# One derived weight of a transformed causal convolution, moved from VectorE to a ScalarE copy and an accumulating DMA

## The chip, the core and the metric

The kernel runs on one core of a Trainium2 chip. The metric is device time in microseconds (us), the median of several executions. TensorE (PE in the profile, with its weight loads listed apart as PEld) multiplies matrices into PSUM; VectorE (DVE) and ScalarE (ACT) do elementwise work; GpSimd (POOL) issues most loads, and SyncE (SP) issues stores and transposing transfers. The engines run their own instruction lists in order and wait for one another through semaphores.

## The reference

```python
def setup_inputs():
    B, S, D, K = 8, 4096, 512, 8
    ...x: (B, S, D) float32, kernel: (K, D, D) float32...

def reference(x, kernel):
    out = np.zeros_like(x)
    for k in range(K):
        if k == 0:
            shifted = x
        else:
            shifted = np.concatenate([np.zeros((B, k, D), dtype=np.float32), x[:, :-k, :]], axis=1)
        out += np.matmul(shifted, kernel[k])
    return out.astype(np.float32)
```

It is a causal convolution over the sequence with eight taps, where each tap is a 512x512 matrix: eight shifted copies of x, each multiplied by its own matrix, are added up.

## The kernel before

The sequences are cut into 128 runs, one to a partition, of 256 positions each. A run is worked off in 32 steps of K = 8 positions. In each step an 8x8 Toeplitz product of 512x512 blocks is to be formed, and the kernel saves multiplications in the manner of Karatsuba, three levels deep: a step has three nodes, `LO`, `HI` and `MID`, instead of four quarter products, and within a node the same is done twice more. For this it needs weights that are differences of taps. There are 27 weight tiles `W[a, b, c]`, each index one of `LO`, `HI`, `MID`, and each tile 128 partitions by 4x512 values in bf16 (512 KB). Eight of them are the taps themselves, loaded by `load_w`, with the cast from float32 in the transfer. A tile with a `MID` in it is the difference of two others, formed on VectorE by `mid_dve(level, u, v)`; the function `mid` gives the result and the two operands. `mid_dve(0, HI, LO)` forms `W[MID,HI,LO] = W[HI,HI,LO] - W[LO,HI,LO]`. Three readers come after it: `mid_dve(1, MID, LO)` at L469 (which gives `W[MID,MID,LO]`), `mid_dve(2, MID, HI)` (which gives `W[MID,HI,MID]`), and the product `node_l(nodes[4], 1, LO)` on TensorE.

x is loaded in halves of four positions by `load_x(i, h)` into a pool of two buffers named `xin`, issued by GpSimd with a cast to bf16. It is transposed into `XT`, in the first steps by TensorE (`transpose_pe`), later by a transposing DMA (`transpose_x`, issued by SP). A load into a buffer waits until the transposes that read the buffer's former content are done: `load_x(2, 1)` at L421 waits for `transpose_x(1, 1)`. VectorE forms the sums of positions in `D4`, `D42`, `D421` and so on, which TensorE takes as its stationary operand.

A node is a series of products of four matmuls each (`product`, L191): `node_a1` and `node_a0` (weights `W[a, MID, ...]`), `node_u`, `node_v` (weights `W[a, b, MID]`) and `node_l`. In between, ScalarE copies PSUM halves (`node_seed`, `node_dts`, the copy in `node_a1`), and VectorE subtracts in PSUM (`node_d`, L76 or L266). `node_l(n, b, HI)` adds to the half that `node_d(n, b)` has read, so it waits for that `node_d`.

The order of all instructions is written by hand (`tc.manual_schedule()`): each engine works off its part of the program text in the order written. The text of the first two steps (six nodes, L330 to L560 or so) mixes products, weight differences, sums and loads one by one, because in this stretch the weights are still arriving or being formed. From the third step on a regular loop follows. The names of all elementwise lines in the profile are those of helpers: L76 is `tt`, every tensor-tensor operation on VectorE, whatever it computes. The profile's `w` is any weight tile.

The first two steps also use some weight tiles that are still free as scratch (`E4`, `T4`, `T42`, `C0`, `C1`). `W[MID,HI,LO]` and its two operands are not among these.

Of the kernel before, what the change touches and what calls it, by code (L numbers as in the profile page):

```python
# [18 lines left out]
LO, HI, MID = 0, 1, 2  # L19
# [3 lines left out]
def kernel(  # L23
# [6 lines left out]
    nc = tc.nc  # L30
# [10 lines left out]
    ADD = mybir.AluOpType.add  # L41
# [14 lines left out]
    W = {}  # L56
# [18 lines left out]
    def tt(o, a, b, op):  # L75
        nc.vector.tensor_tensor(out=o, in0=a, in1=b, op=op)  # L76


    def load(out, src):
        nc.gpsimd.dma_start(out=out, in_=src)  # L80
# [3 lines left out]
    def load_x(i, h):  # L84
        xin[i, h] = xpool.tile([P, 4, D], bf, name="xin")
        load(xin[i, h], xr[:, K * i + 4 * h:K * i + 4 * h + 4, :])
# [31 lines left out]
    def prep_d42(h):  # L118
        if h == LO:
            tt(pairs(D42)[:, 0:2], pairs(D4)[:, 3::-3], pairs(D4)[:, 0:2], ADD)  # L120
        else:
            tt(D42[:, 4:8], D4[:, 2:6], D4[:, 4:8], ADD)
# [11 lines left out]
    def pair(k):  # L134
        return ppool.tile([P, 2, D], f32, name=f"pp{k}")
# [13 lines left out]
    def load_w(tap):  # L149
        n = K - 1 - tap  # L150
        load(W[n >> 2, n >> 1 & 1, n & 1], kr[:, :, tap, :])

    def mid(level, u, v):

        if level == 0:
            return W[MID, u, v], W[HI, u, v], W[LO, u, v]
        if level == 1:
            return W[u, MID, v], W[u, HI, v], W[u, LO, v]
        return W[u, v, MID], W[u, v, LO], W[u, v, HI]

    def mid_dve(*which):
        o, u, v = mid(*which)
        tt(o, u, v, SUB)

    load_w(4)
    load_h(-7, -4)
# [9 lines left out]
    def transpose_pe(name, k, src, t0, t1):  # L176
        o = pair(k).bitcast(bf).rearrange("p a (b d) -> p (a b) d", b=2)
        for t in range(t0, t1):
            for c in range(DC):
                nc.tensor.transpose(o[:, t - t0, c * P:(c + 1) * P], src[:, t, c * P:(c + 1) * P],  # L180
                                    ident)
        bank[name] = o[:, 0:t1 - t0]
# [75 lines left out]
    def node_v(n, b_):  # L258
        product(n.p[b_][:, 1], n.s[2][b_], W[n.a, b_, MID], False)

    def node_d(n, b_):
        p = n.p[b_]
        if b_ == LO:
            tt(p[:, 0], n.dts, p[:, 1], SUB)
        else:
            nc.vector.scalar_tensor_tensor(out=p[:, 0], in0=p[:, 1], scalar=-1.0,  # L266
                                           in1=n.dts, op0=MUL, op1=SUB)
# [48 lines left out]
    def direct(m, t):  # L316
        n = K // 2 - 1 - m
        product(n0.p[t // 2][:, t % 2], D4[:, t - m] if t >= m else E4[:, 4 + t - m],
                W[LO, n >> 1, n & 1], m == 0)
# [42 lines left out]
    tt(D1, XF[:, 3:5], XF[:, 4:6], ADD)  # L362
    direct(1, 2)
    mid_dve(1, LO, HI)
    load_x(1, 0)
    direct(1, 1)
    mid_dve(2, LO, HI)
    tt(F21, D2[:, 0:4], D2[:, 1:5], ADD)
    load_w(0)
    mid_dve(1, LO, LO)  # L370
    mid_dve(2, LO, LO)
    direct(2, 3)
    mid_dve(2, LO, MID)
    transpose_pe("x1", 2, xin[0, 1], 0, 4)
    nc.vector.tensor_copy(out=XT[:, 4:8], in_=bank["x1"])  # L375
    tt(D4[:, 4:8], XF[:, 4:8], XT[:, 4:8], ADD)
# [42 lines left out]
    node_l(nodes[1], 0, HI)  # L419
    node_v(nodes[1], 1)  # L420
    load_x(2, 1)  # L421
    node_d(nodes[1], 1)
    mid_dve(2, HI, MID)
    prep_d421(HI)
# [19 lines left out]
    node_a1(3)  # L444
    node_l(nodes[2], 0, LO)
    mid_dve(0, LO, LO)
    mid_dve(0, HI, LO)
    prep_d42(HI)
    node_l(nodes[2], 0, HI)
    node_a0(nodes[3])  # L450
# [182 lines left out]
```

## Time and profile before

| what | value |
|---|---|
| time, median of 4 runs | 782.47 us (781.68 to 782.84) |
| the profiled execution | 782.99 us, span of its instructions 781.1 us |
| busy, PE | 765.1 us (98% of the span), 3505 matmuls recorded |
| busy, DVE | 660.6 us (85%) |
| busy, ACT | 280.7 us (36%) |
| busy, POOL | 41.8 us (5%) |
| DMA | 138.37 MB, mean 177 GB/s |
| mean granted TensorE clock | 0.993 |

The span is what lies between the first and the last instruction; the profiled execution's own time is 1.9 us more. Busy time of PE is the sum of modelled instruction spans, and following matmuls overlap in it, so a busy share of 98% doesn't mean that PE has only 2% to win or lose. The stretches of interest are the first 65 us; after it the loop repeats with each step of three nodes.

### The profile page before, as it was taken

How to read it: one execution, taken by the hardware profiler on the slowest of the kernel's cores; microseconds unless marked ns; L12 is line 12 of the kernel's file. 1: busy time of each engine (PE TensorE's matmuls, PEld its weight loads, DVE VectorE, ACT ScalarE, POOL GpSimd, SP SyncE). 2: the span in 40 equal slices, each digit the busy share in tenths (PEclk: the TensorE clock that was granted, in tenths of full speed). 3: DMA queues.
4: the chain of work that ended last, by engine and by line, in shares of the span. 5: the costliest groups of instructions: out<-in, count | busy, mean ns of one | idle time of the engine just before them, and what ended most of it. 6: DMA issues, size and time to landing. Idle time of an engine off the chain costs nothing.

```text
span 781.1 us, 9348 instructions
## 1 busy us (share of the span) xinstructions
PE 765.1 (98%) x3505; PEld 348.7 (45%) x3576; DVE 660.6 (85%) x768; ACT 280.7 (36%) x459; POOL 41.8 (5%) x80
## 2 busy tenths in 40 slices
PE   7999999999999999999999999999999999999997
PEld 3444444444444444444444444444444444444443
DVE  3999988888888898888898888888888898888895
ACT  1453433333343324343333333333343333343332
POOL 4000000000000000000000000000000000000000
PEclk7999999999999999999999999999999999999999
DMA  9946978777787787787687787878697867788843
GB/s 163 210 79 154 246 169 212 172 179 173 178 177 196 174 185 176 172 190 187 163 196 178 165 202 176 198 159 187 168 189 178 206 163 186 164 181 179 205 130 124
DMA packets 159229, 138.37 MB, mean 177 GB/s; under 512 B 130130, under 2 KB 134226, under 8 KB 159184
## 3 DMA queue, kind: packets, MB, share of 16 engines
q1 hardware_dynamic: 145312, 98.84, 45.7%
q0 software_dynamic: 13728, 38.66, 30.7%
q8 instruction: 28, 0.46, 0.2%
q10 hardware_dynamic: 144, 0.26, 0.1%
q14 instruction: 17, 0.14, 0.1%
HBM read 77.32 MB, written 67.11 MB: 185 GB/s over the span
## 4 chain that ended last, share of the span: by engine, by line
PE 91%; DVE 5%; DMA 2%; issue 1%; ACT 0%; DVEq 0%; POOL 0%; SPq 0%; ACTq 0%; POOLq 0%
PE pp L191 91%; DVE D L76 2%; DVE w L76 2%; DMA XT<-xin 1%; DMA xin<-in_x_dram 1%; DVE y L76 1%; PE pp L180 1%; DVE pp L76 0%; DVE pp L266 0%; DVE XT L375 0%; ACT D L341 0%; ACT D L342 0%; DVE D L334 0%; POOL D L80 0%; DVEq L628 0%
## 5 line engine op out<-in xcount | busy, mean ns | idle before, releaser
L191 PE MATMUL pp<-w,D 128*128 128x512 bf16 x3213 | 714.4, 380 | 5.8 <-ACT D L342 1.2
L191 PEld LDWEIGHTS <-D 128*128 128x128 bf16 x3280 | 320.7, 98 | 392.4 <-issue 5.6
L76 DVE TENSOR_TENSOR D<-D 128x1024 bf16<-128x1024 bf16 x252 | 228.4, 946 | 0.4 <-issue 0.2
L76 DVE TENSOR_TENSOR y<-pp,ms 128x1024 f32<-128x1024 f32 (+1 forms) x121 | 146.4, 1211 | 45.7 <-PE pp L191 44.1
L76 DVE TENSOR_TENSOR D<-XT 128x2048 bf16<-128x2048 bf16 (+2 forms) x153 | 142.3, 946 | 12.3 <-DMA XT<-xin 10.7
L238 ACT COPY pp<-pp 128x512 f32<-128x512 f32 x95 | 54.1, 570 | 254.9 <-PE pp L191 252.1
L250 ACT COPY pp<-pp 128x512 f32<-128x512 f32 x95 | 54.2, 571 | 163.7 <-PE pp L191 151.7
L76 DVE TENSOR_TENSOR pp<-dts,pp 128x512 f32<-128x512 f32 x95 | 65.5, 690 | 43.1 <-ACT dts L256 41.8
L293 ACT COPY ms<-pp 128x1024 f32<-128x1024 f32 x60 | 61.0, 1016 | 34.9 <-PE pp L191 30.6
L80 POOL DMA_DIRECT2D xin<-in_x_dram x64 | 33.9, 530 | 690.7 <-DMA XT<-xin 673.4
L266 DVE SCALAR_TENSOR_TENSOR pp<-pp,dts 128x512 f32<-128x512 f32 x95 | 65.9, 693 | 3.3
L256 ACT COPY dts<-pp 128x512 f32<-128x512 f32 x95 | 57.5, 606 | 4.2 <-PE pp L191 4.2
L252 ACT ACTIVATE pp<-pp 128x512 f32<-128x512 f32 x95 | 56.0, 589 | 2.1 <-DVE D L76 2.1
L191 PE MATMUL pp<-w,XT 128*128 128x512 bf16 x118 | 30.5, 379 | 0.1
L76 DVE TENSOR_TENSOR w<-w,w 128x2048 bf16<-128x2048 bf16 x19 | 22.6, 1218 | 0.0
L191 PEld LDWEIGHTS <-XT 128*128 128x128 bf16 x120 | 11.7, 98 | 14.2
L191 PE MATMUL pp<-w,w 128*128 128x512 bf16 x34 | 8.8, 379 | 0.8 <-ACT pp L250 0.7
L191 PE MATMUL pp<-w,F 128*128 128x512 bf16 x36 | 8.6, 379 | 0.0
L174 PE MATMUL pp<-zero 128*128 128x512 bf16 x16 | 6.3, 554 | 1.2 <-DVE zero L145 1.2
L180 PE MATMUL pp<-ident,xin 128*128 128x128 bf16 x48 | 4.2, 249 | 3.1 <-DMA xin<-in_x_dram 1.9
L334 DVE COPY D<-pp 128x1024 bf16<-128x1024 bf16 x1 | 0.7, 691 | 7.1 <-PE pp L180 7.1
L378 ACT COPY w<-XT 128x1024 bf16<-128x1024 bf16 x1 | 1.0, 1045 | 14.3 <-DVE XT L375 14.3
(52 smaller groups left out, 74.9 us busy)
## 6 DMA issues: line engine op xcount, KB each, us to landing
out_dram<-y SPq DMA_DIRECT2D x123, 512.0 KB, 3.3
xin<-in_x_dram POOLq DMA_DIRECT2D x64, 512.0 KB, 5.5
w<-in_kernel_dram POOLq DMA_DIRECT2D x8, 512.0 KB, 16.6
out_dram<-ms SPq DMA_DIRECT2D x2, 512.0 KB, 6.6
out_dram<-f SPq DMA_DIRECT2D x2, 512.0 KB, 9.0
XT<-xin SPq DMA_TRANSPOSE x61, 6.2
D<-in_x_dram POOLq DMA_DIRECT2D x1, 508.0 KB, 5.5
D<-in_x_dram POOLq DMA_DIRECT2D x1, 381.0 KB, 11.1
```

The lines of the kernel that those rows point to most:

```text
L76: nc.vector.tensor_tensor(out=o, in0=a, in1=b, op=op)
L80: nc.gpsimd.dma_start(out=out, in_=src)
L174: nc.tensor.matmul(pw[:, h], lhsT=zero[:, 0:P], rhs=zero, start=True, stop=True)
L180: nc.tensor.transpose(o[:, t - t0, c * P:(c + 1) * P], src[:, t, c * P:(c + 1) * P], ident)
L191: nc.tensor.matmul(bank, lhsT=comp[:, c * P:(c + 1) * P], rhs=w[:, c, :], start=start and c == 0, stop=c == DC - 1, skip_group_check=True)
L238: nc.scalar.copy(out=n.q[:, 0], in_=n.q[:, 1])
L250: nc.scalar.copy(out=n.p[b_][:, 1], in_=n.q[:, 1])
L252: nc.scalar.mul(out=n.p[b_][:, 1], in_=n.q[:, 1], mul=-1.0)
L256: nc.scalar.copy(out=n.dts, in_=n.q[:, 0])
L266: nc.vector.scalar_tensor_tensor(out=p[:, 0], in0=p[:, 1], scalar=-1.0, in1=n.dts, op0=MUL, op1=SUB)
L293: nc.scalar.copy(out=ms[b_], in_=p)
L378: nc.scalar.copy(out=C0[:, 0:2], in_=XT[:, 6:8])
```

## The change

`mid_dve(0, HI, LO)` is taken out of VectorE's list. In its place there are two instructions. ScalarE writes the negated `W[LO,HI,LO]` into `W[MID,HI,LO]`, at a place in the text just before the first transposes of `xin[0, 1]`. Later GpSimd issues one DMA, from SBUF to SBUF, that adds `W[HI,HI,LO]` to what stands in `W[MID,HI,LO]`; it stands in the text right behind `load_x(2, 1)`, so GpSimd gets to it once that load has been issued, which is once the transposes of the second step's upper half (`transpose_x(1, 1)`) are done. The weight comes out the same: `W[HI,HI,LO] - W[LO,HI,LO]` in bf16.

```diff
     def mid_dve(*which):
         o, u, v = mid(*which)
         tt(o, u, v, SUB)
+
+
+    def mid_neg(u, v):
+        nc.scalar.mul(out=W[MID, u, v], in_=W[LO, u, v], mul=-1.0)
+
+    def mid_acc(u, v):
+        nc.gpsimd.dma_start(out=W[MID, u, v], in_=W[HI, u, v], accum_op=ADD)
 ...
     mid_dve(2, LO, LO)
     direct(2, 3)
     mid_dve(2, LO, MID)
+    mid_neg(HI, LO)
     transpose_pe("x1", 2, xin[0, 1], 0, 4)
 ...
     node_v(nodes[1], 1)
     load_x(2, 1)
+    mid_acc(HI, LO)
     node_d(nodes[1], 1)
 ...
     mid_dve(0, LO, LO)
-    mid_dve(0, HI, LO)
     prep_d42(HI)
```

## The prediction

> **What bounds the kernel now.** I read the page first, its busy shares and its chain of work by engine.
>
> ```profile
> PE 765.1 (98%) x3505; PEld 348.7 (45%) x3576; DVE 660.6 (85%) x768; ACT 280.7 (36%) x459; POOL 41.8 (5%) x80
> PE 91%; DVE 5%; DMA 2%; issue 1%; ACT 0%; DVEq 0%; POOL 0%; SPq 0%; ACTq 0%; POOLq 0%
> ```
>
> TensorE carries nine tenths of the chain, so a removed VectorE instruction is worth only what TensorE stops waiting for. VectorE's 5% lies in one stretch, which the chain in order of time shows (start, length, what), here cut to 45 to 66 us:
>
> ```profile
> 48.73 2.26 DVE w L76 x2
> 50.99 1.14 DVE D L76
> 52.12 0.06 DVE pp L266
> 52.18 0.46 issue
> 52.64 1.21 DVE D L76
> 53.85 1.14 DVE w L76
> 54.99 0.33 DVE A L76
> 55.32 1.15 DVE w L76
> 56.47 0.05 issue
> 56.52 3.63 PE pp L191 x16
> ```
>
> Up to 56.5 VectorE leads and TensorE follows; from there TensorE leads, with 0.05 us pieces that recur every 10.8 us to the end and so hang on no dependency. The instruction to be removed is the second of the pair at 48.73. How long TensorE really waits is in the stage table by single microseconds (PE, PEld, DVE, ACT, POOL busy, clock, DMA share, GB/s):
>
> ```profile
> 48.00:49.00 1.00, 0.83 (x4) 0.41 (x5) 1.00 (x3) 0.00 (x0) 0.00 (x0) 1.00 1.13 229
> 52.00:53.00 1.00, 0.88 (x5) 0.29 (x3) 1.00 (x3) 0.97 (x2) 0.00 (x0) 1.00 0.00 0
> 56.00:57.00 1.00, 0.88 (x5) 0.25 (x4) 1.00 (x3) 0.56 (x1) 0.00 (x0) 1.00 0.03 8
> 62.00:63.00 1.00, 0.95 (x5) 0.23 (x4) 1.00 (x2) 1.00 (x3) 0.00 (x0) 1.00 0.50 92
> ```
>
> A visible gap is smaller than the delay, because listed matmuls overlap. TensorE's timeline gives the rate: 16 in a row last 3.62 us, so with 0.379 us for the last one, 15 steps take 3.24 us, 0.216 us each; 0.379 - 0.216 = 0.163 us of each step is overlap.
>
> ```profile
> 23.07 3.62 PE L191 MATMUL pp<-w,D 128*128 128x512 bf16 x16
> ```
>
> So the gaps of 0.12, 0.12 and 0.05 us at 52.8, 56.5 and 62.8 delay TensorE by about 0.28, 0.28 and 0.21 us. The gap at 48 lies ahead of the removed instruction and stays.
>
> **What is removed.** VectorE's timeline:
>
> ```profile
> 48.63 2.35 DVE L76 TENSOR_TENSOR w<-w,w 128x2048 bf16<-128x2048 bf16 x2
> 57.58 1.22 DVE L76 TENSOR_TENSOR w<-w,w 128x2048 bf16<-128x2048 bf16 x1
> 61.50 2.36 DVE L76 TENSOR_TENSOR w<-w,w 128x2048 bf16<-128x2048 bf16 x2
> ```
>
> Two take 2.35 us, one 1.22, so the second is worth 1.13 us of VectorE's time. VectorE has no idle time from there to 65 us, so everything behind moves up by 1.13 us while its inputs allow.
>
> Follow the waits. At 52.79 `node_l(nodes[2], 1, HI)` waits for `node_d(nodes[2], 1)`, which ended at 52.04 + 0.69 = 52.73 and now ends near 51.6; TensorE gets there at 52.79 - 0.28 = 52.51. Gone: 0.28. At 56.52 `node_a1(4)` waits for `W[MID,MID,HI]` (55.24 + 1.22 = 56.46), now ready at 55.33; TensorE arrives at 56.52 - 0.56 = 55.96. Gone: another 0.28. At 62.78 `node_v(nodes[4], 0)` waits for `W[MID,LO,MID]`, first of the pair at 61.50, now done near 61.6, while TensorE arrives at 62.78 - 0.21 - 0.56 = 62.0. But this product also needs the seed copy, which ends on ScalarE at 61.96 + 0.58 = 62.54 and moves up only with TensorE, by 0.56, to about 61.98. So little is kept there: I count 0.15 of 0.21. What is late next is TensorE itself; two small waits behind (its weight loader's waits for `F` near 73.3 and 75.9, some 0.1 us each) may lose 0.04. Sum: 0.28 + 0.28 + 0.15 + 0.04 = 0.75 us.
>
> **The negated copy.** ScalarE's timeline:
>
> ```profile
> 28.88 1.04 ACT L378 COPY w<-XT 128x1024 bf16<-128x1024 bf16 x1 [14.25 <-DVE XT L375]
> 31.95 1.90 ACT L391 COPY w<-XT 128x2048 bf16<-128x2048 bf16 x1
> ```
>
> A copy of this shape takes 1.90 us. It stands in ScalarE's list just ahead of the copy at 28.88, before which ScalarE idles 14.25 us. It waits for tap 5, which VectorE already reads in the pair of differences that starts at 20.66, so it runs at about 22 to 24 us at the latest, 5 us before anything queued behind it. Counted at nothing. Without that cover it would hold up the copies of `XT` behind it by up to 1.9 us, and with them VectorE's `T4` sum.
>
> **The accumulating DMA.** GpSimd's timeline:
>
> ```profile
> 45.29 0.53 POOL L80 DMA_DIRECT2D xin<-in_x_dram  x1 [14.50 <-DMA XT<-xin]
> 63.62 0.53 POOL L80 DMA_DIRECT2D xin<-in_x_dram  x1 [17.80 <-DMA XT<-xin]
> ```
>
> It is issued at 45.82 and takes 0.5 to 0.8 us of GpSimd (`load_x` and `load_w` rows). It waits for the copy (done by 24) and for tap 1, whose load left at 17.06 and lands in at most 20.6 us, 37.7. Only `load_x(3, 0)` is queued behind it, at 63.62 after 17.80 us of idling: nothing. The transfer follows `load_x(2, 1)` on the same queue:
>
> ```profile
> DMA  0000000099992547499891989939699190000000
> xin<-in_x_dram POOLq DMA_DIRECT2D x1, 512.0 KB, 4.9
> ```
>
> This is the DMA view of 45.5 to 50.5 us in slices of 0.125: the load moves from 46.5 to 49.6 (3.1 us) and lands at 45.29 + 4.9 = 50.2. Then the DMA engines are idle until the transposes issued at 58.77 (the 52 to 53 row above has 0 GB/s). No row shows an accumulate. Lower bound: it runs beside the load as quickly as a 512 KB store, 3.3 us, landing at 49.1. Upper bound: it starts when the load has landed and takes twice its 4.9, because the destination is read too: 50.2 + 9.8 = 60.0. The load row is nearest, since it also reads 1 MB (float32) and writes 512 KB: 49.6 + 3.1 + 0.6 for landing = 53.3.
>
> The first reader is `mid_dve(1, MID, LO)`, at 57.58 before, now due at 56.45. A landing by 56.85 costs nothing (the 0.4 us that `W[MID,LO,MID]` has over TensorE); at 57.58 VectorE is where it was before and the gain is lost at 62.78; from there each microsecond late costs one, since VectorE's whole list queues behind that wait. At 53.3 there are 3.5 us to spare: nothing.
>
> The Trainium skill has a price for the add: Collectives: The Full Stack, section The bandwidth ceiling, says that the add itself is free and the second read halves the rate, some 31 GB/s per engine; 32 KB an engine would take 2.1 us (an estimate from that page), and the sum would be the same. A rule that speaks against the change is in SBUF — State Buffer, Summary: don't hide a GpSimd-issued DMA under VectorE work, since descriptor writing is starved in VectorE's fast modes. Here VectorE was busy without a break while GpSimd issued at 45.29 in its usual 0.53 us. By the rule one more VectorE instruction, 1.22 us, would pass first: a landing at 54.5, and the same sum.
>
> **Rivals.**
> *No gain.* TensorE meets the next wait at once (ScalarE's seeds at 62), and the time stays 782.5. For it: the seed's end at 62.54 against 62.78. Against: TensorE is still 0.56 us earlier when it gets there, and those seeds follow TensorE.
> *A late landing, slower.* The accumulate takes more than 57.58 - 45.82 = 11.8 us from issue. It passes 0.2% from a landing at 59.1. At the upper bound of 60.0 VectorE is 2.4 us later than before: 784.9. If it were as slow as the slowest `xin` load (17.8 us to landing, under load), it lands at 63.6: 788.5. For it: no row shows an accumulate. Against: idle engines for 10 us.
> *Faster by over 0.2%.* This needs 1.56 us, more than VectorE gives up. All waits to 76 us make 0.28 + 0.28 + 0.21 + 0.2 = 0.97; the break in TensorE's chain at 692.6, where the stage table shows 0.48 us without a matmul (0.48 + 0.16 = 0.64), would have to vanish too: 1.61, 780.9.
>
> **How the numbers follow.** The profiled execution's 782.99 us (span 781.1 and 1.9 around it) would become 782.24. It lies 0.52 above the median of the runs shown, so I set the sum against the median: 782.47 - 0.75 = 781.7. Chances: forecast 0.52, no gain 0.20, late landing 0.18, over 0.2% faster 0.10. About 0.2% (1.56 us) is what a measurement of this kernel can tell from no change, so: faster 0.10, same 0.72, slower 0.18. The range goes up to the late landing's upper bound, 784.9, and down to 780.7, the forecast less most of the runs' own scatter (1.0 of 1.16); this leaves out the farther late landings and part of the last rival.
>
> **What would show it.** A ScalarE instruction of 1.9 us near 20 to 24; a DMA of GpSimd at 45.8 landing near 53; VectorE's next `w` difference starting at about 56.4 without idle time; no TensorE gap at 52.5 and 56, and the periodic matmul pattern from 63 on some 0.7 us earlier. Wrong if VectorE idles at 56.4 with that DMA as releaser, or if TensorE's gaps are merely moved.

## The result, and the profile after

The changed kernel takes 781.53 us (median of 39 runs, 780.93 to 783.83) against 782.65 us of the kernel before (57 runs, 781.52 to 783.8). The ratio is 0.9987 with a 95% interval of 0.9982 to 0.9991: a gain of 1.0 us, between 0.7 and 1.4. A ratio of 1 lies outside that interval, and the gain is under the 0.2% that was named as the bound for no change. The forecast was 781.7: its sum of 0.75 us was set against 782.47, the median of the 4 runs of before that it had.

The page of the changed kernel, with its busy times, its chain by engine, and the row of the new transfer:

```profile
PE 763.4 (98%) x3505; PEld 348.1 (45%) x3576; DVE 659.6 (85%) x767; ACT 282.5 (36%) x460; POOL 42.7 (5%) x81
PE 93%; DVE 4%; DMA 1%; issue 1%; ACT 0%; POOL 0%; DVEq 0%; ACTq 0%; POOLq 0%
w<-w POOLq DMA_DIRECT2D x1, 512.0 KB, 10.0
```

VectorE has one instruction less, ScalarE and GpSimd one more each, and the chain has moved from VectorE to TensorE. The chain in order of time shows where:

```profile
46.94 0.70 DVE D L76
47.65 0.05 issue
47.70 0.60 PE pp L198 x2
48.30 0.05 issue
48.35 4.70 PE pp L198 x21
53.05 0.03 issue
53.08 6.20 PE pp L198 x28
```

TensorE now leads from 47.7 us, where it led from 56.5. (This profile runs 0.48 us earlier than the one shown of before already at 47.7, ahead of everything that the removed instruction can touch. A second profile of before, e4 below, is 0.73 us earlier than the first; the start scatters.) The stage table has the same columns as before, PE first:

```profile
52.00:53.00 1.00, 1.00 (x5) 0.39 (x4) 1.00 (x2) 0.97 (x3) 0.00 (x0) 1.00 1.05 209
53.00:54.00 1.00, 0.97 (x6) 0.44 (x5) 1.00 (x3) 1.00 (x3) 0.00 (x0) 1.00 0.87 176
56.00:57.00 1.00, 1.00 (x7) 0.43 (x5) 1.00 (x2) 1.00 (x2) 0.00 (x0) 1.00 0.03 8
62.00:63.00 1.00, 1.00 (x6) 0.44 (x5) 0.74 (x2) 0.19 (x1) 0.16 (x1) 1.00 0.00 0
692.00:693.00 1.00, 1.00 (x7) 0.44 (x5) 0.89 (x2) 0.00 (x0) 0.00 (x0) 1.00 0.89 229
```

The gaps of 0.12, 0.12 and 0.05 us are gone. With 0.16 us of overlap each they stood for 0.28 + 0.28 + 0.21 us. One new gap of 0.03 at 53.1 stands for 0.19. So 0.58 us are gained in this stretch. The last row holds a second gain that the forecast did not count: before, this microsecond had

```profile
692.00:693.00 1.00, 0.52 (x3) 0.19 (x2) 1.00 (x2) 1.00 (x3) 0.00 (x0) 1.00 1.02 197
```

a gap of 0.48, that is 0.64 us of delay. Now there is none. 0.58 + 0.64 = 1.2 us, which is within the interval of the times. The starts of the matmuls, compared one by one between the two profiles, agree: the changed kernel moves ahead by 0.57 us between 47.5 and 64 us, and by 0.63 us at 692.

The new instructions, from the timelines of ScalarE, GpSimd and VectorE (start, length, instruction, idle time before it):

```profile
19.21 1.91 ACT L167 ACTIVATE w<-w 128x2048 bf16<-128x2048 bf16 x1 [4.92 <-DMA w<-in_kernel_dram]
28.40 1.05 ACT L386 COPY w<-XT 128x1024 bf16<-128x1024 bf16 x1 [7.27 <-DVE XT L383]
46.34 0.91 POOL L170 DMA_DIRECT2D w<-w  x1
55.07 0.70 DVE L273 SCALAR_TENSOR_TENSOR pp<-pp,dts 128x512 f32<-128x512 f32 x1 [0.23 <-PE pp L198]
55.68 0.69 DVE L76 TENSOR_TENSOR pp<-dts,pp 128x512 f32<-128x512 f32 x1
56.32 1.22 DVE L76 TENSOR_TENSOR w<-w,w 128x2048 bf16<-128x2048 bf16 x1
```

The copy runs at 19 to 21 us in ScalarE's idle time. The accumulate is issued at 46.34 and lands 10.0 us later, at 56.3. `mid_dve(1, MID, LO)` starts at 56.32, which is 0.64 us after the subtraction ahead of it, where 0.60 is usual. It was hidden, but with nothing to spare. VectorE had lost time just before, too: at 55.07 a `node_d` waited for TensorE. So `mid_dve(1, MID, LO)` comes 8.17 us after the first difference (48.15), and not the 7.82 that 57.58 - 48.63 - 1.13 makes; without that wait it would have been due at 55.97, 0.3 us ahead of the landing.

### The profile page after: what moved, and what is told of

It is laid out like the page before. It is cut to its first block, busy times and chain, and to the rows that moved or that the text cites. A ratio compares the mean times of both kernels' runs of the same rounds, so it can differ in the third digit from the quotient of the medians.

```text
span 779.3 us, 9350 instructions
## 1 busy us (share of the span) xinstructions
PE 763.4 (98%) x3505; PEld 348.1 (45%) x3576; DVE 659.6 (85%) x767; ACT 282.5 (36%) x460; POOL 42.7 (5%) x81
## 4 chain that ended last, share of the span: by engine, by line
PE 93%; DVE 4%; DMA 1%; issue 1%; ACT 0%; POOL 0%; DVEq 0%; ACTq 0%; POOLq 0%
PE pp L198 93%; DVE w L76 2%; DVE D L76 1%; DMA xin<-in_x_dram 1%; PE pp L187 0%; DVE XT L383 0%; DVE F L76 0%; ACT D L348 0%; ACT D L349 0%; DVE D L341 0%; DVE y L76 0%; DVE pp L76 0%; POOL D L80 0%; DVE pp L273 0%; DVEq L636 0%
## 5 line engine op out<-in xcount | busy, mean ns | idle before, releaser
L80 POOL DMA_DIRECT2D w<-in_kernel_dram x8 | 6.1, 766 | 2.1 <-DMA w<-in_kernel_dram 1.8
```

## The experiments

**Without the DMA** (e1_neg_only). Is it VectorE's time that was gained, and does the DMA cost anything?

```diff
     load_x(2, 1)
-    mid_acc(HI, LO)
     node_d(nodes[1], 1)
```

> The ScalarE copy stays, VectorE's difference stays away, and the accumulating DMA is left out too, so W[MID,HI,LO] holds only -W[LO,HI,LO]. Theory (the gain is VectorE's 1.13 us, and the DMA, landing at 56.3 where its first reader is due at 56.3, hides just completely): the same as the changed kernel, 781.5, within 0.2 us; VectorE's mid_dve(1, MID, LO) again starts about 8.2 us after the first difference at 48.15. Rival A (the landing already binds and costs part of the gain): 781.1 or less, with mid_dve(1, MID, LO) a few tenths earlier. Rival B (the gain comes from what the DMA does to the queues or to the phase of later transfers, not from VectorE): back to 782.6.

Measured: 781.55 us (11 runs), ratio to before 0.9985 (0.9977 to 0.9994): the changed kernel's time. VectorE's timeline:

```profile
48.65 1.22 DVE L76 TENSOR_TENSOR w<-w,w 128x2048 bf16<-128x2048 bf16 x1
56.77 1.22 DVE L76 TENSOR_TENSOR w<-w,w 128x2048 bf16<-128x2048 bf16 x1
```

The distance is 8.12 us, against 8.17 in the changed kernel (48.15 to 56.32). So the landing held VectorE up by 0.05 us at most, and the DMA as such brings and costs nothing. Rivals A and B fall.

**A landing that is late** (e2_acc_twice). What does lateness cost?

```diff
     mid_acc(HI, LO)
+    mid_acc(HI, LO)
```

> A second accumulating DMA of the same operand into the same tile follows the first and has to wait for its landing, so the tile holds 2 W[HI,HI,LO] - W[LO,HI,LO]. Theory (past the break-even landing each microsecond costs one): the second is issued at about 56.4, takes 0.9 us to issue and, alone on the DMA engines, some 6.5 us more to land, near 63.7; mid_dve(1, MID, LO) starts there instead of 57.1 (its place in the kernel before, on this clock), so 6.6 us slower than before: 789.2. Rival (other VectorE and TensorE work covers part of it, because VectorE has idle time again after 62 us): under 786.

Measured: 787.02 us (785.74 to 789.18, 4 runs), ratio 1.0066 (1.0051 to 1.0082). Slower, but by 4.4 us and not 6.6. GpSimd's timeline, and VectorE's:

```profile
45.98 0.91 POOL L170 DMA_DIRECT2D w<-w  x1
54.92 0.86 POOL L170 DMA_DIRECT2D w<-w  x1 [8.04 <-DMA w<-w]
59.84 1.22 DVE L76 TENSOR_TENSOR w<-w,w 128x2048 bf16<-128x2048 bf16 x1 [3.73 <-DMA w<-w]
```

The second accumulate, alone on the DMA engines, lands 4.9 us after its issue, as a load does. (VectorE is idle while it moves, from 56.1 to 59.84, so this run doesn't tell whether a busy VectorE would lengthen it.) I had expected 7.4, so the landing was misjudged. The price was misjudged too. The second profile of before (e4 below), whose start agrees with this one within 0.03 us, has this difference at 56.84, so the lateness is 3.0 us. Matmul by matmul, TensorE is 0.4 us ahead of e4 before the wait and 4.2 us behind it at 64 us; later, at 692, it gets 0.5 back. (The two profiled executions, 785.74 and 782.11, lie 3.6 us apart; the 4.4 between the medians rests on four runs of this kernel, which scatter by 3.4.) The stage table shows what is added (the number behind the five engines is the granted clock):

```profile
59.00:60.00 1.00, 0.00 (x0) 0.00 (x0) 0.17 (x1) 0.00 (x0) 0.00 (x0) 1.00 0.84 156
61.00:62.00 1.00, 0.88 (x4) 0.41 (x6) 1.00 (x3) 0.00 (x0) 0.00 (x0) 1.00 0.79 149
62.00:63.00 1.00, 0.95 (x3) 0.34 (x3) 1.00 (x2) 0.59 (x1) 0.10 (x1) 0.62 0.00 0
63.00:64.00 1.00, 1.00 (x4) 0.42 (x3) 0.97 (x3) 0.31 (x1) 0.45 (x1) 0.50 0.00 0
64.00:65.00 1.00, 1.00 (x4) 0.32 (x3) 1.00 (x2) 0.70 (x1) 0.00 (x0) 0.50 0.91 66
65.00:66.00 1.00, 1.00 (x4) 0.38 (x3) 1.00 (x1) 0.55 (x2) 0.00 (x0) 0.68 0.93 188
```

No matmul runs for 3.0 us, from 58.15 to 61.12. The clock is still full when the matmuls begin again; it goes down to 0.5 at 62.2 and is back about 3.4 us later. What the last four rows lack in clock, 0.38 + 0.5 + 0.5 + 0.32, is 1.7 us, and 3.0 + 1.7 - 0.4 = 4.3 is close to the 4.2 measured. So that lateness costs one for one does not hold here.

**The DMA earlier** (e3_acc_early). Does its place behind the transposes matter?

```diff
     load_x(2, 0)
+    mid_acc(HI, LO)
     node_d(nodes[1], 0)
 ...
     load_x(2, 1)
-    mid_acc(HI, LO)
```

> The accumulating DMA stands behind load_x(2, 0) instead of load_x(2, 1), so it is issued as soon as tap 1 has landed, at about 37.7, and is queued behind the loads that end at 42.6. Theory (the place behind the transposes matters because the transfer shares the DMA engines with transpose_x(1, 1) at 41.8 to 44.8, whose result VectorE needs at 45.6): the weight lands by 50, the transposes land 0.5 to 1.5 us later, prep_d4(HI) starts that much later and TensorE's wait at 47.7 grows: 782.0 to 783.0. Rival (the transposes keep their pace, and the earlier landing gives slack but no gain): 781.5.

Measured: 783.24 us (11 runs), ratio 1.0012 (1.0003 to 1.0021): slower than before, by a little more than expected. GpSimd's, VectorE's and TensorE's timelines:

```profile
38.82 0.89 POOL L170 DMA_DIRECT2D w<-w  x1 [8.00 <-DMA w<-in_kernel_dram]
47.76 1.23 DVE L76 TENSOR_TENSOR D<-XT 128x2048 bf16<-128x2048 bf16 x1 [1.53 <-DMA XT<-xin]
49.84 2.33 PE L198 MATMUL pp<-w,D 128*128 128x512 bf16 x9 [1.74 <-DVE D L76]
```

The accumulate is off GpSimd at 39.7 and lands in 7.0 us, but `transpose_x(1, 1)` takes 6.9 us instead of 4.8, VectorE waits 1.53 us for it, and TensorE 1.74. The same DMA is free behind these transposes and costs 1.7 us beside them (783.24 - 781.53).

**The kernel before once more** (e4_before_again; no edit).

> The kernel before once more, for a second profile of it. Theory: TensorE waits again at about 52.8, 56.5 and 62.8 us for VectorE (0.28, 0.28, 0.21 us of delay); the start up to 47.7 us and the break at 692 us are scatter that need not come again. Rival (the break of 0.64 us at 692 belongs to the kernel before, and its absence is a part of the gain): it is there again.

The one execution took 782.11 us. The gaps between 52 and 62 us are there (with this early start at 52.06, 55.79 and 62.06), and so is the one at 692:

```profile
691.00:693.00 2.00, 1.50 (x8) 0.58 (x6) 1.98 (x5) 1.58 (x3) 0.00 (x0) 1.00 1.01 178
```

0.50 of TensorE's time is missing, as in the first profile, while the three profiles above and the changed kernel's show no gap at that place. The rival stands: this gap belongs to the kernel before, and its absence is a part of the gain. The forecast had it only in a rival of 10%. The prediction read the chain of before as TensorE's from 56.5 us to the end, but at this place it runs through a transposing DMA, VectorE and ScalarE (cut):

```profile
682.04 7.40 DMA XT<-xin
...
690.68 1.23 DVE y L76
691.98 0.58 ACT pp L250
692.60 5.99 PE pp L191 x27
```

What goes along with it is seen in the DMA view of the transposes that begin just after 682 (kernel before, 682.4 to 689.9 us; queue and kind, packets, MB, share, and in the last line the us to landing):

```profile
q8 instruction: 1, 0.02, 0.9%
q14 instruction: 1, 0.01, 0.6%
...
XT<-xin SPq DMA_TRANSPOSE x1, 7.4
```

and in the changed kernel, 681.2 to 688.3 us:

```profile
q8 instruction: 1, 0.02, 0.8%
...
XT<-xin SPq DMA_TRANSPOSE x1, 6.8
```

In the kernel before, an 8 KB instruction fetch (q14) falls into the transposes, which take 7.4 us instead of 6.8. In the changed kernel it comes 1 us before they begin. VectorE waits for these transposes, and TensorE, with no room left at this place, waits for VectorE by way of a ScalarE copy. The changed kernel has one instruction more on ScalarE; the next two runs separate that from VectorE's lead.

**The copy without the gain** (e5_copy_and_dve), and **the gain without the copy** (e6_plain_no_act).

```diff
     load_x(2, 1)
-    mid_acc(HI, LO)
 ...
     mid_dve(0, LO, LO)
+    mid_dve(0, HI, LO)
```

> ScalarE's negated copy stays, but VectorE's difference is back (it overwrites the copy) and the accumulating DMA is gone: the kernel before with one more ScalarE instruction. In the two profiles of before the transposes that begin near 682 us take 7.4 us and TensorE loses 0.64 us at 692; in all four kernels with the copy and without VectorE's difference they take 6.8 and nearly nothing is lost; an 8 KB instruction fetch falls into the transposes in the first two and ahead of them in the others. Theory 1 (one more ScalarE instruction moves that fetch forward): TensorE's waits at 52.8, 56.5 and 62.8 are as before, and the loss at 692 is gone: 782.0. Theory 2 (VectorE's lead, not the instruction count, decides): the loss at 692 is there, 782.6. Rival (the loss at 692 was scatter): either, not tied to the fetch.

```diff
     def mid_acc(u, v):
-        nc.gpsimd.dma_start(out=W[MID, u, v], in_=W[HI, u, v], accum_op=ADD)
+        nc.gpsimd.dma_start(out=W[MID, u, v], in_=W[HI, u, v])
 ...
     mid_dve(2, LO, MID)
-    mid_neg(HI, LO)
```

> The negated copy is left out, and the DMA copies W[HI,HI,LO] into W[MID,HI,LO] without adding, so the tile holds W[HI,HI,LO] alone; VectorE's difference stays away. Theory 1: TensorE gains its 0.56 us between 47 and 63, but with ScalarE's instruction count as before the fetch falls into the transposes and the 0.6 us at 692 are lost again: 782.1. Theory 2: as the changed kernel, 781.5. A plain copy reads one operand less than the accumulate; if that is what lengthened the landing to 10.0 us beside load_x(2, 1), it lands in 8 us or less, if sharing the queue is, in 9 to 10.

Measured: e5 782.25 us (11 runs), ratio 0.9998 (0.9989 to 1.0007); e6 782.04 us (11 runs), ratio 0.9997 (0.9988 to 1.0006). Both lie between the two kernels, as halves of the gain would, but neither is told apart from no change by its times. The traces do tell them apart. Stage table of e5, two rows:

```profile
56.00:57.00 1.00, 0.88 (x5) 0.30 (x4) 1.00 (x3) 0.61 (x1) 0.00 (x0) 1.00 0.03 8
692.00:693.00 1.00, 1.00 (x6) 0.48 (x5) 0.98 (x3) 0.79 (x2) 0.00 (x0) 1.00 1.12 197
```

and of e6, whose gap lies 1 us earlier:

```profile
56.00:57.00 1.00, 1.00 (x7) 0.43 (x5) 1.00 (x3) 0.70 (x1) 0.00 (x0) 1.00 0.02 8
691.00:692.00 1.00, 0.75 (x5) 0.28 (x3) 1.00 (x2) 0.92 (x2) 0.00 (x0) 1.00 0.98 180
```

e5 waits for VectorE at 56 as the kernel before does, and loses nothing at 692. e6 doesn't wait at 56, and loses at 691 (0.25 + 0.16 = 0.41 us). The DMA views agree: in e6 the fetch lies in the transposes, which take 7.2 us; in e5 it lies ahead of them, and they take 6.8. Theory 1 holds in all ten profiles: with the extra ScalarE instruction 6.8 or 6.9 us, without it 7.2 to 7.4. e6 changes two things, the copy and the add, but e1 and e5, without any such DMA, have the fetch ahead, so it is the copy that decides. The rates agree: in the quarter of a microsecond that begins 2.75 us after the transposes are issued, 36 to 54 GB/s are moved in the three profiles with the fetch inside, and 210 to 220 in the other seven. What the profile doesn't name is the engine that the fetch is for; that it is ScalarE is inferred from the edits that move it. How the fetch slows the transposes isn't shown either: it comes some 2 us ahead of the low rate.

e6 also shows a plain copy beside `load_x(2, 1)`: 7.2 us to landing, 0.54 us of GpSimd. The load ahead of it lands after 6.3 us, and after 6.6 to 6.8 ahead of an accumulate (the changed kernel, e2, e7, e8), against 4.8 to 5.2 with nothing behind it (before, e1, e4, e5). So the two transfers slow each other, and adding lengthens the second one's landing further (8.7 to 10.0 us, 0.91 us of GpSimd).

**A further step** (e7_swap_e), and **the changed kernel once more** (e8_after_again; no edit).

```diff
     node_u(nodes[3])
-    node_e(nodes[2], 0)
     node_e(nodes[1], 1)
+    node_e(nodes[2], 0)
     node_seed(nodes[3], 0)
```

> The changed kernel with two ScalarE copies swapped (node_e(nodes[1], 1) ahead of node_e(nodes[2], 0)), so that the seed copy for node_v(nodes[3], 0) needn't wait for both. Theory: the 0.19 us that TensorE still loses at 53.1 in the changed kernel belongs to that seed (its copy ends at 52.46 + 0.57 = 53.03): the delay goes, 781.3, a difference that shows in the trace rather than in the times. Rival: TensorE's loss there has another cause and stays: 781.5.

> The changed kernel once more, for a second profile: the landing of the accumulate against the due time of its first reader. Theory: 9 to 10 us from issue to landing, and mid_dve(1, MID, LO) waits for nothing or a few hundredths of a microsecond; no loss at 692. Rival: the landing is later than due in some executions by more than 0.3 us, and TensorE waits again near 60.

Measured: e7 781.58 us (11 runs), ratio 0.9988 (0.9979 to 0.9997), not to be told from the changed kernel. Its trace shows the step taken, in ScalarE's timeline and in the stage table:

```profile
52.84 0.57 ACT L257 COPY pp<-pp 128x512 f32<-128x512 f32 x1 [0.77 <-PE pp L198]
49.00:62.00 13.00, 13.00 (x62) 5.87 (x61) 12.92 (x16) 8.16 (x13) 0.00 (x0) 1.00 0.53 95
```

The seed now waits for TensorE alone, and TensorE has no gap in 13 us. So the 0.19 us that the changed kernel lost at 53.1 were the seed's. A gain of 0.2 us is too small for these runs to show in the time. e8 took 781.12 us: its accumulate is issued at 45.93 and lands in 8.8 us, at 54.7; the first reader starts at 56.06, so here there are 1.4 us to spare. TensorE loses nothing at 692. The changed kernel's two landings, 10.0 and 8.8 us (8.8 in e7 too, and 8.7 for the first one in e2), differ by more than the slack that the first profile left.

## Why the prediction was right, point by point

- **VectorE's 1.13 us are worth what TensorE stops waiting for.** Right: 0.58 us between 48 and 63, of 0.71 foreseen. The waits at 52.8, 56.5 and 62.8 went as described; what was missing is the seed copy. I named ScalarE's seeds as what is late next, but placed the loss at 62 (0.06) and not at 53.1, where it is 0.19, as e7 shows. At 62.8 nearly all of the 0.21 went, and the 0.04 near 73 and 76 did not come: between 64 and 78 us the matmuls of the changed kernel gain nothing. VectorE's lead was 1.13 us only up to 55; then it waited for TensorE, and 0.8 were left.
- **The negated copy costs nothing.** Right: it ran at 19.2 to 21.1 in ScalarE's idle time. It did have an effect that no step of mine had: it moved an instruction fetch that comes 660 us later (e5, e6).
- **The accumulating DMA is hidden.** Right in its sign (e1), wrong in its size. I foresaw a landing at 53.3 and 3.5 us to spare; it lands 8.8 to 10.0 us after the issue, at 54.7 to 56.3, with 0 to 1.4 to spare. The landing by 56.85 that was to cost nothing is 56.37 on the clock of the first profile, so there it was met by 0.1 us. The term that was mis-sized is the 3.1 us of a further transfer set behind the load: alone, and with VectorE idle, the accumulate does land in 4.9 us, its packets moving in 3.0 (e2; the prediction's other estimate was 2.1), but next to the load both are slowed. In the changed kernel the two together move from 47 to 56 us, and in the DMA view of 46 to 57 us the load needs 6.8 us to its landing instead of 4.9. The 0.5 to 0.8 us of GpSimd were 0.91.
- **Past the break-even a microsecond costs a microsecond.** Not so: 3.0 us late put TensorE 4.2 us behind the kernel before, because of its clock (e2).
- **The break at 692.** I took it for a place that might or might not vanish, and kept it out of the sum. It vanishes in every profile with the negated copy, and is about half of the gain. The forecast of 0.75 came near the measured 1.0 by leaving out 0.64 there and counting 0.17 too much before. That the time came within 0.2 us of 781.7 is luck in part: against 782.65, the median of the 57 runs, the same sum gives 781.9.

The rule on GpSimd-issued DMAs under VectorE work (the Trainium skill, SBUF — State Buffer, Summary) would have had the descriptor writing starved. VectorE worked with hardly a break at all of these issues, and the load took its usual 0.53 us and the accumulate 0.86 to 0.91 us at three different places, so the rule doesn't show. (VectorE was at its faster rate at the load's issue and at that of the changed kernel's accumulate: there it had bf16 instructions of 2048 elements, 1.2 us each, as long as its float32 ones of 1024.) An accumulate issued under an idle VectorE was not tried. Whether VectorE's work lengthens the landing is open, since the one accumulate that landed in 4.9 us moved while VectorE was idle; a load lands in 4.8 to 5.2 us beside a busy VectorE.

## What to carry to other kernels

Work moved from a leading engine is worth the waits it ends, one by one, up to the next wait of another kind; the copy and the DMA in its place cost nothing here, since the copy stood where its engine was idle and the DMA landed just in time. Here the place of the transfer decided more than its length: it is free behind a transposing DMA that is awaited, and costs more than the whole gain beside it. When a time moves by a tenth of a per cent, look for a second cause far from the edit: here an added instruction moved an instruction fetch as well.

## What the runs showed of the hardware that I had not expected

- An 8 KB instruction fetch inside a transposing DMA goes along with 7.2 to 7.4 us for that transfer instead of 6.8 or 6.9 (ten profiles), and where there is no room that reaches TensorE (0.4 to 0.6 us).
- 3.0 us without matmuls were followed by a granted clock of 0.5 for about 3.4 us (e2). The Trainium skill, TensorE: Matmul & The Clock Gate, Part 1, describes a gate with windows of about 3.4 us after which an idle TensorE runs at half speed; the recovery agrees, while here 3.0 us of idling were enough. How long is too long these runs don't settle: 1.7 us without matmuls left the clock at 1.00 in e3 (48.10 to 49.84), while some 1.8 us near the start of every profile (7.46 to 9.31 in the kernel before) were followed by 0.5.
- Two GpSimd-issued transfers of 512 KB one after the other on one queue slow each other: 4.8 to 5.2 us to landing for the load alone and 4.9 for the accumulate alone (e2, with VectorE idle), 6.6 to 6.8 and 8.7 to 10.0 together.
